# SSM inputs brought into step order: one wide copy and transfers through DRAM in place of sixteen small copies a chunk

## The chip, the cores and the metric

The kernel runs on one core of one Trainium2 chip. The metric is the device time of one execution in microseconds. The core's engines run side by side, each through its own queue of instructions in order: TensorE (PE in the profile, PEld for its weight loads), VectorE (DVE), ScalarE (ACT), GpSimd (POOL) and SyncE (SP), which here only issues transfers (DMA). An engine waits at an instruction until what it needs is there, and everything behind it on that queue waits too.

## What is computed

One decoder block over 512 tokens of width 1024: a conditioned norm, one combined input projection, differential attention beside a diagonal state space model (SSM), gates, an output projection, and a mixture of 32 experts. The change lies in the SSM branch; cut to it, the reference is:

```python
h = modulate(rms_norm(x, norm1_g), shift1, scale1)
q, k, v, u, gates = split(h @ w_in)            # u: (512 tokens, 512 channels)
ug = u.reshape(1, 512, 32, 16)                 # 32 groups of 16 channels
bu = einsum('bsgh,gph->bsgp', ug, bb)          # complex, 64 states a group
x_t = a * x_(t-1) + bu_t                       # scan over the 512 tokens, per state
y = Re(einsum('bsgp,ghp->bsgh', x, c)) + d_skip * ug
y = gelu(y); gl = y @ w_glu
y_ssm = gl[:, :512] * sigmoid(gl[:, 512:])
merged = g_attn * (y_attn @ w_proj_attn) + g_ssm * (y_ssm @ w_proj_ssm)
```

## The kernel before

The 512 SSM channels are worked on in four chunks `c` of 128. The SSM goes four tokens at a time: token 4b + q is step q of block b, with 128 blocks. For that the input of a chunk has to lie in "step order": the tile `us` (`U[c]`, 128 x 4 x 128) has in partition 32q + h channel h of a quarter of the chunk at step q, and in its free part the quarter j and the block b. The input projection leaves u differently: channel on the partition, tokens in order along the free part, in the PSUM tiles `acc` 0 to 3. `ssm_u(c)` (line 415) does the rearrangement with 16 copies of 32 x 128 on ScalarE (line 420), each reading every fourth token. Chunk 0 is read straight from PSUM; chunks 1 to 3 are first copied into SBUF tiles `u1` to `u3` (line 574).

`ssm_steps` (line 704) then takes each chunk through these steps: `ssm_rotate` (matmuls `bu` of `us` with `W`, line 652, then the products `m` and sums `z` on VectorE with tables `cos` and `sin`), `ssm_in` for the next chunk (its `ssm_u`, then transposes `bt` on TensorE, line 428, and copies `W` on ScalarE, line 429), `ssm_scan`, `ssm_back` (`xri`) and, one chunk later, `ssm_y` (matmuls `yp`, lines 692 and 694, the latter reading `us` again; then a table load and 16 GELU instructions `yf`, line 698). `us` has two buffers, so chunk c + 2 can be filled only when `yp` of chunk c has been computed. `table` builds `cos` and `sin` for the next chunk on VectorE and ScalarE.

Beside this TensorE works through the rest of the input projection: `acc` (line 180; q, k) and value matmuls `vps` (line 185), whose weights arrive as `ws` (line 145, 512 KB each), are cast by ScalarE to `wh` (line 153), and the remainder `wl` is formed by VectorE (a line 90). Every few matmuls a "tick" runs one SSM step or one unit of the second conditioning product (`ada_unit`): a 512 KB transfer `adaw` (line 747) and 8 matmuls `mvb` (line 749). Units 0 to 15 use two buffers of `adaw`, later ones four; every eighth unit ends with a VectorE step `mr` and a small transfer `mrd`. `tv` (line 768), `tvd` and `bsd` (lines 770 and 772) build the table of attention biases through DRAM; `bsd` is 1 MB from DRAM to DRAM, and `B` (line 777) reads it.

From line 566 on a scheduler decides the order of the instructions on each engine, up to the attention stage, where TensorE's order is written out by hand. Its order is fixed when the program is built; the transfers of SP are one queue in that order too.

```python
uT = [acc[0]]
for c in range(1, 4):
    uT.append(t1(f"u{c}", [128, T]))
    S.copy(uT[c], acc[c])
    if c == 1:
        ssm_u(0)
```

Of the kernel before, what the change touches and what calls it, by code (L numbers as in the profile page):

```python
# [9 lines left out]
F32 = mybir.dt.float32  # L10
# [9 lines left out]
T, D = 512, 1024  # L20
# [37 lines left out]
def hybrid_block(ctx: ExitStack, tc: tile.TileContext, x, cols, cst, ada_a, ada_b, b_rows, bc_rows, lamv, relb,  # L58
                 onehot, units, rw, rb, bpad, cpad, w_ein, w_eout, out):
    nc = tc.nc  # L60
    V, S, G, TE = nc.vector, nc.scalar, nc.gpsimd, nc.tensor
# [3 lines left out]
    dram = ctx.enter_context(tc.tile_pool(name="dram", bufs=1, space=DRAM))  # L65

    def bank(i, shape=(128, 512), name=None):
        return psum.tile(list(shape), F32, tag=f"b{i}", name=name or f"bank{i}")
# [8 lines left out]
    def t1(tag, shape, dt=F32, name=None):  # L77
        pool = late if tag[:-1] == "tmp" else mid if tag[:-1] in ("BT", "CT", "sgA", "xs") else early
        return pool.tile(list(shape), dt, tag=tag, name=name or tag)
# [116 lines left out]
    def two(i, name):  # L196
        if i == 0:
            return [bank(0, name=name), bank(1, name=name)]
        t = pair(name=name)
        return [t[:, 0], t[:, 1]]  # L200
# [114 lines left out]
    v, y, t = (st4[:, j] for j in range(3))  # L315
# [97 lines left out]
    U, W = {}, {}  # L413

    def ssm_u(c):

        U[c] = t1(f"v{c % 2}", [128, 4, 128], name="us")
        for j in range(4):
            for q in range(4):
                S.copy(U[c][32 * q:32 * q + 32, j], uT[c][32 * j:32 * j + 32, q::4])  # L420

    def ssm_w(c, ps):

# [95 lines left out]
    with tc.manual_schedule(engines={mybir.EngineType.PE, mybir.EngineType.DVE, mybir.EngineType.Activation}):  # L519
# [4 lines left out]
        acc = two(0, "acc0") + two(1, "acc2") + [bank(m, name=f"acc{m}") for m in (4, 5)]  # L524
# [11 lines left out]
        for k in range(KC):  # L536
            first, second = unit_parts(UNITS[k]) if k in UNITS else (lambda: None, ) * 2
            for n in range(3 * 6):

                m, w = (n // 2, n % 2) if n < 12 else (n - 12, 2)  # L540
                b = 6 * k + m
# [26 lines left out]
    for _ in setup:  # L568
        pass

    uT = [acc[0]]
    for c in range(1, 4):
        uT.append(t1(f"u{c}", [128, T]))
        S.copy(uT[c], acc[c])
        if c == 1:
            ssm_u(0)
    qT, kT, vt = [None] * 4, [None] * 4, [None] * 4

# [61 lines left out]
    def ssm_in(c):  # L640
        if c:
            ssm_u(c)
            ps = pair((128, 2, 4, 128), "bt")
            ssm_w(c, [ps[:, ri] for ri in range(2)])
# [325 lines left out]
    for i in range(4):  # L970
        m2s = []
        for m in (2 * i, 2 * i + 1):
# [6 lines left out]
            b = t1(f"u{2 + m % 2}", [128, T], name="mb")  # L979
# [5 lines left out]
        for j in range(2):  # L985
            cs = slice(256 * i + 128 * j, 256 * i + 128 * j + 128)
            v = m2s[j].rearrange("p (i t) -> p i t", t=128)
# [826 lines left out]
```

## Time and profile before

| | |
|---|---|
| median of 3 runs | 939.51 us (938.96 to 942.91) |
| the profiled execution | 938.94 us, its span 937.1 us |
| TensorE busy | 893.2 us (95% of the span), 4967 matmuls |
| VectorE busy | 502.0 us (54%) |
| ScalarE busy | 300.3 us (32%), 616 instructions |
| GpSimd busy | 2.2 us |
| moved by DMA | 268.70 MB, mean 287 GB/s |
| 61.5 to 200 us | the SSM beside q, k, v and the conditioning |
| 200 to 323 us | attention with gates between |
| 450 to 921 us | experts |

Busy shares are means over stages of very different kinds: in the experts' stage TensorE is busy 468.0 of 471 us. What counts for a change in one stage is which waits end last there. Matmuls are pipelined, so the busy time of TensorE contains no small gaps; a wait that shows is a real one. The granted clock of TensorE is given as a share of 2.4 GHz.

### The profile page before, as it was taken

Reading aid. Unit: us, or ns where it says so; the run is one execution under the profiler, and the core shown is the slowest. Engines: PE = TensorE matmul, PEld = TensorE weight load, DVE = VectorE, ACT = ScalarE, POOL = GpSimd, SP = SyncE. Lnnn points to the kernel's source line nnn. Section 1 sums busy time; section 2 is a strip of 40 time slices with the busy share of each in tenths; the row PEclk is TensorE's granted clock in tenths of the full one; section 3 lists DMA queues with packets and bytes.
Section 4 is the critical chain, followed back from the end, with each engine's and each line's share of the span. In section 5 each row is a group of like instructions: output and inputs, shape, how many; then the busy total and the mean of one; then the engine's idle time right before and its main releaser. Section 6 shows DMA issues by size and latency. Waiting matters only on the chain.

```text
span 937.1 us, 12889 instructions
## 1 busy us (share of the span) xinstructions
PE 893.2 (95%) x4967; PEld 554.4 (59%) x4967; DVE 502.0 (54%) x1256; ACT 300.3 (32%) x616; POOL 2.2 (0%) x8
## 2 busy tenths in 40 slices
PE   8997997889999999999999999999999999999994
PEld 4775765567778788778455543555435554355343
DVE  7896685656765557469524432544225442244336
ACT  4565568895644433243201000010000100001014
POOL 0000000000000000000000000000000000000000
PEclk9998999999999999999999999999999999999998
DMA  9925765612222623691899999999999999999952
GB/s 362 376 82 175 253 219 194 218 55 86 68 68 69 220 94 126 262 376 40 343 379 417 420 420 420 420 420 420 420 420 420 420 420 419 420 420 420 419 174 93
DMA packets 77590, 268.70 MB, mean 287 GB/s; under 512 B 5535, under 2 KB 11567, under 8 KB 77524
## 3 DMA queue, kind: packets, MB, share of 16 engines
q1 hardware_dynamic: 77524, 267.82, 72.9%
q8 instruction: 41, 0.67, 0.3%
q14 instruction: 25, 0.20, 0.1%
HBM read 265.68 MB, written 3.17 MB: 287 GB/s over the span
## 4 chain that ended last, share of the span: by engine, by line
PE 83%; ACT 6%; DVE 6%; DMA 3%; issue 1%; SPq 0%; DVEq 0%; ACTq 0%
PE hid L1412 23%; PE yb L1419 11%; PE acc L180 11%; PE cb L1397 7%; PE xg L1155 6%; PE pAS L180 5%; PE po L185 4%; PE acc L543 4%; DMA adaw<-ada_b 3%; ACT us L420 3%; PE plg L180 2%; ACT yf L698 2%; PE pv L864 1%; PE lp L1088 1%; PE mv L474 1%
## 5 line engine op out<-in xcount | busy, mean ns | idle before, releaser
L1412 PE MATMUL hid<-w,xT 128*64 128x512 f32 x1024 | 222.9, 592 | 0.0
L1412 PEld LDWEIGHTS hid<-w,xT 128*64 128x64 f32 x1024 | 73.3, 137 | 145.3 <-issue 136.5
L1419 PE MATMUL yb<-w,sa 128*64 128x512 f32 x480 | 106.3, 595 | 0.0
L90 DVE TENSOR_TENSOR sa<-sa,hid 128x512 f32<-128x512 f32 (+1 forms) x17 | 11.1, 656 | 166.3 <-PE hid L1412 153.9
L90 DVE TENSOR_TENSOR wl<-ws,wh 128x1024 fp32r<-128x1024 f32 x52 | 63.5, 1223 | 56.1 <-ACT wh L153 45.4
L90 DVE TENSOR_TENSOR x<-x,cb 128x512 f32<-128x512 f32 (+1 forms) x132 | 79.9, 664 | 2.0 <-PE cb L1397 2.0
L153 ACT ACTIVATE wh<-ws 128x1024 fp32r<-128x1024 f32 x51 | 53.7, 1057 | 80.0 <-PE acc L180 24.5
L180 PE MATMUL acc<-hh,wh 128*128 128x512 f32 x176 | 74.1, 421 | 4.4 <-ACT wh L153 4.4
L1390 ACT CAST yh<-yf 128x512 fp32r<-128x512 f32 x29 | 17.9, 619 | 172.0 <-DVE yf L96 141.7
L1419 PEld LDWEIGHTS yb<-w,sa 128*64 128x64 f32 x480 | 33.2, 137 | 65.0 <-issue 64.4
L180 PE MATMUL acc<-hl,wh 128*128 128x512 f32 x176 | 70.9, 403 | 0.0
L180 PE MATMUL acc<-hh,wl 128*128 128x512 f32 x176 | 70.6, 402 | 0.0
L1377 ACT ACTIVATE sa<-hid 128x512 f32<-128x512 f32 x15 | 9.0, 597 | 177.0 <-PE hid L1412 177.0
L96 DVE SCALAR_TENSOR_TENSOR yf<-yb,ws,gate 128x512 f32<-128x512 f32 x29 | 21.8, 751 | 80.8 <-PE yb L1419 80.3
L1155 PE MATMUL xg<-P,mh 128*128 128x256 f32 x224 | 54.7, 284 | 0.0
L1155 PE MATMUL xg<-P,ml 128*128 128x256 f32 x224 | 53.5, 280 | 0.0
L1397 PE MATMUL cb<-yh,PT 128*128 128x512 f32 x116 | 48.2, 416 | 0.4 <-ACT yh L1390 0.3
L1397 PE MATMUL cb<-yl,PT 128*128 128x512 f32 x116 | 45.9, 396 | 2.1 <-DVE yl L90 2.0
L1155 PEld LDWEIGHTS xg<-P,ml 128*128 128x128 f32 x224 | 42.2, 189 | 0.5
L1155 PEld LDWEIGHTS xg<-P,mh 128*128 128x128 f32 x224 | 42.1, 188 | 0.5
L180 PEld LDWEIGHTS acc<-hh,wh 128*128 128x128 f32 x176 | 33.7, 191 | 14.1 <-ACT wh L153 4.6
L180 PEld LDWEIGHTS acc<-hh,wl 128*128 128x128 f32 x176 | 33.5, 190 | 9.4 <-issue 1.6
(316 smaller groups left out, 1441.3 us busy)
## 6 DMA issues: line engine op xcount, KB each, us to landing
w<-w_ein SPq DMA_DIRECT2D x128, 1024.0 KB, 13.3
w<-w_eout SPq DMA_DIRECT2D x63, 1024.0 KB, 17.5
ws<-units SPq DMA_DIRECT2D x52, 512.0 KB, 3.6
adaw<-ada_b SPq DMA_DIRECT2D x32, 512.0 KB, 4.5
ada<-ada_a SPq DMA_DIRECT2D x8, 512.0 KB, 8.2
ada<-ada_a SPq DMA_DIRECT2D x16, 256.0 KB, 7.1
X<-x SPq DMA_DIRECT2D x4, 512.0 KB, 6.4
x<-x SPq DMA_DIRECT2D x4, 512.0 KB, 5.5
```

The source lines that it names most:

```text
L90: return emit(o, lambda: (eng or V).tensor_tensor(o, a, b, op=op))
L96: return emit(o, lambda: V.scalar_tensor_tensor(o, a, s, b, op0=op0, op1=op1, **k))
L153: return (lambda: S.activation(hi, st, AF.Copy) if u else V.tensor_copy(hi, st)), lambda: tt(lo, st, f32(hi), OP.subtract)
L180: TE.matmul(o, a, b, start=start and i == 0, stop=stop and i == 2)
L185: TE.matmul(o, a, b, start=start and i == 0, stop=stop and i == 2)
L420: S.copy(U[c][32 * q:32 * q + 32, j], uT[c][32 * j:32 * j + 32, q::4])
L543: TE.matmul(acc[m], (hi, lo, hi)[w], hT(k)[w // 2], start=k == 0 and n < 12 and w == 0, stop=k == KC - 1 and w == 2)
L698: S.activation(f[32 * j:32 * j + 32, p::4], yp[32 * p:32 * p + 32, j], AF.Gelu_apprx_tanh)
L1155: TE.matmul(o, (h2h, h2l)[w][i][:, 128 * k:128 * k + 128], P[:, i].rearrange("p a b -> p (a b)"), start=start, stop=i == NT - 1 and w == 1 ...
L1397: TE.matmul(ps, PT if len(y) == 2 else f32(PT), a, start=w == 0, stop=w == len(y) - 1)
L1412: m = TE.matmul(hid[q][64 * e:64 * e + 64], xT[p, k // 4][:, k % 4, 64 * e:64 * e + 64], ring[p][k][:, e, 512 * q:512 * q + 512], start=k ...
L1419: TE.matmul(yb[q][64 * e:64 * e + 64], hT_[:, f, 64 * e:64 * e + 64], ring[p][8 + f][:, e, 512 * q:512 * q + 512], start=f == 0, stop=f == ...
```

## The change

`ssm_u` no longer copies. After the projection each chunk, chunk 0 now too, is copied once from PSUM to an SBUF tile `u` with the tokens regrouped by step (128 x 512, read with a step of four). ScalarE issues a 256 KB transfer of it into a DRAM tile `ud`. `ssm_u(c)` is four 64 KB transfers on SP's queue, one for each step q, which read the 32 channels of all four quarters from DRAM in runs of 128 elements into the 32 partitions of `us` that belong to q.

```diff
     def ssm_u(c):
 
         U[c] = t1(f"v{c % 2}", [128, 4, 128], name="us")
-        for j in range(4):
-            for q in range(4):
-                S.copy(U[c][32 * q:32 * q + 32, j], uT[c][32 * j:32 * j + 32, q::4])
+        v = ud[c].rearrange("(j h) (q b) -> q h j b", h=32, b=128)
+        for q in range(4):
+            nc.sync.dma_start(U[c][32 * q:32 * q + 32], v[q])
...
-    uT = [acc[0]]
-    for c in range(1, 4):
-        uT.append(t1(f"u{c}", [128, T]))
-        S.copy(uT[c], acc[c])
-        if c == 1:
+    ud = []
+    for c in range(4):
+        u_ = t1(f"u{c}", [128, T], name="u")
+        S.copy(u_.rearrange("p (q b) -> p q b", q=4), acc[c].rearrange("p (b q) -> p q b", q=4))
+        ud.append(dram.tile([128, T], F32, name=f"ud{c}"))
+        nc.scalar.dma_start(ud[c], u_)
+        if c == 0:
             ssm_u(0)
```

The scheduler puts this together anew. ScalarE's queue right after the input projection stands before the change as (`us` from `acc_281` is chunk 0, from `u_866` chunk 1; `wh_919` and `wh_1029` are the first two weight tiles of the next projections):

```order
L420 COPY us<-acc_281 32x128 x4
L574 COPY u_866<-acc_282 128x512
L420 COPY us<-acc_281 32x128 x12
...
L420 COPY us<-u_866 32x128 x6
L768 COPY tv<-tvp 4x320
L420 COPY us<-u_866 32x128 x10
L919 ACT_TABLE_LOAD
L919 ACTIVATE lmt<-lmt 128x2
L581 ACTIVATE q_1024<-acc 128x512
L768 COPY tv<-tvp 4x320
L153 ACTIVATE wh_919<-ws_917 128x1024
L153 ACTIVATE wh_1029<-ws_1027 128x1024
```

After the change the same place reads as follows (`ud_868` to `ud_885` are the stores of chunks 0 to 3):

```order
L574 COPY u<-acc_281 128x512
L574 COPY u<-acc_282 128x512
L576 DMA ud_868<-u 128x512
L576 DMA ud_877<-u 128x512
L574 COPY u<-acc_283 128x512 x2
...
L576 DMA ud_881<-u 128x512
L576 DMA ud_885<-u 128x512
L770 COPY tv<-tvp 4x320
L921 ACT_TABLE_LOAD
L921 ACTIVATE lmt<-lmt 128x2
L583 ACTIVATE q_1010<-acc 128x512
L770 COPY tv<-tvp 4x320
L153 ACTIVATE wh_917<-ws_915 128x1024
```

The 32 small copies are gone from in front of the second `tv` and of `wh`, and two pairs of transfer issues stand there.

SP's queue at the same time, before the change, from the transfers of conditioning units 2 and 3 on:

```order
L747 DMA adaw<-ada_b 128x1024 x2
L145 DMA ws_917<-units 128x1024
L145 DMA ws_1027<-units 128x1024
L770 DMA tvd<-tv 4x640
L747 DMA adaw<-ada_b 128x1024 x2
L145 DMA ws_1110<-units 128x1024
L772 DMA bsd<-tvd 512x1x512
```

And after it:

```order
L749 DMA adaw<-ada_b 128x1024 x2
L420 DMA us<-ud_868 32x4x128 x4
L420 DMA us<-ud_877 32x4x128 x4
L145 DMA ws_915<-units 128x1024
L145 DMA ws_1013<-units 128x1024
L772 DMA tvd<-tv 4x640
L749 DMA adaw<-ada_b 128x1024 x2
L145 DMA ws_1096<-units 128x1024
L774 DMA bsd<-tvd 512x1x512
```

Eight loads of `us` now stand between the two `adaw` and the weight tiles.

TensorE's queue at `yp` of chunk 1, in the second stage, before (the `mvb` x4 and x12 are conditioning units 16 and 17 to 19):

```order
L692 MATMUL yp<-xri,CA 128x128 x2
L749 MATMUL mvb<-adaw,c_94 32x256 x4
L694 MATMUL yp<-us,G 128x128
L749 MATMUL mvb<-adaw,c_94 32x256 x12
L428 MATMUL bt<-colt,BE 128x128 x4
L692 MATMUL yp<-xri,CA 128x128 x2
L694 MATMUL yp<-us,G 128x128
L692 MATMUL yp<-xri,CA 128x128 x2
L694 MATMUL yp<-us,G 128x128
```

And after (the last `mvb` x4 here is unit 20):

```order
L751 MATMUL mvb<-adaw,c_94 32x256 x12
L428 MATMUL bt<-colt,BE 128x128 x4
L696 MATMUL yp<-us,G 128x128
L694 MATMUL yp<-xri,CA 128x128 x2
L696 MATMUL yp<-us,G 128x128
L694 MATMUL yp<-xri,CA 128x128 x2
L751 MATMUL mvb<-adaw,c_94 32x256 x4
L696 MATMUL yp<-us,G 128x128
```

A block of `mvb` has moved to just ahead of the last matmul of `yp`. Elsewhere in this part the order of ScalarE and VectorE is nearly what it was.

## Rows read from the trace of the kernel before

**Rows 1.** Windows by stage: length, then busy time (instructions) of each engine, clock, DMA.
```profile
61.50:105.90 44.40, 37.80 (x227) 26.28 (x226) 31.00 (x67) 25.27 (x55) 0.00 (x0) 0.92 0.58 208
...
132.90:157.00 24.10, 17.44 (x134) 12.29 (x133) 12.14 (x19) 20.50 (x41) 0.00 (x0) 1.00 0.44 148
157.00:178.00 21.00, 16.89 (x97) 12.11 (x95) 13.98 (x24) 20.34 (x42) 0.00 (x0) 0.92 0.64 227
178.00:200.00 22.00, 18.71 (x144) 12.86 (x144) 18.21 (x28) 19.19 (x39) 0.00 (x0) 0.97 0.42 157
200.00:323.00 123.00, 122.75 (x597) 97.65 (x595) 72.19 (x241) 67.01 (x152) 0.00 (x0) 0.99 0.28 94
```

**Rows 2.** TensorE's waits from 61.5 to 200 us: total us, times, longest.
```profile
PE acc L180 <- ACT wh L153: 4.4, 1, 4.4
PE bu L652 <- ACT W L429: 4.1, 1, 4.1
PE bt L428 <- DVE m L90: 3.6, 2, 2.3
PE sc L837 <- DVE qs L90: 3.2, 2, 2.8
PE mvb L749 <- DMA adaw<-ada_b: 2.9, 3, 1.5
PE yp L692 <- ACT yf L698: 1.6, 1, 1.6
PE mvb L749 <- DVE mr L90: 1.3, 1, 1.3
```

**Rows 3.** Line 420: count, ns minimum/median/maximum, first and last start.
```profile
L420 ACT COPY us<-u x48: 408/418/447, 69.3 to 163.6; 32x128 f32<-32x128 f32 x48
L420 ACT COPY us<-acc x16: 252/256/260, 62.5 to 67.1; 32x128 f32<-32x128 f32 x16
```

**Rows 4.** Timeline of the first stage: start us, length us, what, idle before.
```profile
63.53 0.59 ACT L574 COPY u<-acc 128x512 f32<-128x512 f32 x1
...
71.84 0.70 PE L767 MATMUL tvp<-oht,rbt 33*4 33x320 f32 x2
...
78.50 0.40 ACT L768 COPY tv<-tvp 4x320 f32<-4x320 f32 x1
...
78.81 2.00 ACT L153 ACTIVATE wh<-ws 128x1024 fp32r<-128x1024 f32 x2
...
80.63 0.67 SPq L772 DMA_DIRECT2D bsd<-tvd  x1
...
98.07 0.33 SPq L777 DMA_DIRECT2D B<-bsd  x1
```

**Rows 5.** Waits of SP's queue from 60 to 205 us.
```profile
SPq L770 <- ACT tv L768: 12.9, 1, 12.9
```

**Rows 6.** Timeline of ScalarE in the second and third stage.
```profile
132.94 6.93 ACT L420 COPY us<-u 32x128 f32<-32x128 f32 x16 [0.53 <-PE yp L694]
...
157.08 6.92 ACT L420 COPY us<-u 32x128 f32<-32x128 f32 x16 [0.76 <-PE yp L694]
...
170.53 0.59 ACT L429 COPY W<-bt 128x512 f32<-128x512 f32 x1
171.14 1.20 ACT L698 ACTIVATE yf<-yp 32x128 f32<-32x128 f32 x3
```

**Rows 7.** Transfer issues: count, KB each, median us from issue to landing.
```profile
ws<-units SPq DMA_DIRECT2D x52, 512.0 KB, 3.6
adaw<-ada_b SPq DMA_DIRECT2D x32, 512.0 KB, 4.5
...
colt<-cols SPq DMA_DIRECT2D x1, 107.5 KB, 2.0
```

**Rows 8.** Windows of 3 us, columns as in rows 1.
```profile
81.00:84.00 3.00, 1.69 (x7) 1.25 (x6) 3.00 (x6) 0.43 (x1) 0.00 (x0) 0.50 0.96 367
```

**Rows 9.** The chain that ended last, in order of time: start us, length us.
```profile
108.59 6.30 PE acc L180 x27
```

## The prediction

> **What bounds the kernel now.** I first read the windows by stage, for where TensorE is not kept busy [rows 1]. From 200 us on it is (122.75 of 123.00 us in the attention stage). Between 61.5 and 200 us it idles 6.6 us before 105.9, 6.7 us from 132.9 to 157, 4.1 us to 178 and 3.3 us to 200, and its granted clock falls to 0.92 in two of these stretches. So only this front part can give time, and what it gives passes on, since all that follows is released by work that moves with it.
>
> TensorE's waits there have seven entries [rows 2]. Five lead to ScalarE or to something queued behind it: acc on wh (4.4 us), bu on W (4.1), yp on yf (1.6), mvb on mr (1.3; on VectorE mr stands behind wl, which waits for wh), bt on m (3.6 in two waits, 1.3 and 2.3; m stands behind the cosine table and, the first time, behind lmt, both ScalarE results). The other two are sc on qs (3.2) and mvb on adaw transfers (2.9 in three waits, the longest 1.5).
>
> The copies of line 420 are 16 x 0.256 us and 48 x 0.418 us, 24.2 us of ScalarE [rows 3]. In the first stage 32 of them lie between the end of the input projection and the second copy of tv, at 78.50 us, and wh follows at 78.81 [rows 4]. SP, which issues its transfers in order, waited 12.9 us for that tv [rows 5]: nothing was loaded meanwhile. In the second and third stage 16 copies each, 6.93 and 6.92 us, stand directly ahead of the table load and yf [rows 6].
>
> **The change, part by part.** It removes 24.2 us from ScalarE. It adds one 128x512 copy (u of chunk 0; the three others were there, 0.59 us each [rows 4]) and four transfer issues on ScalarE's queue. No strided 512-element copy out of PSUM is in the trace: between 0.59 us (contiguous) and four times 0.256 (four strided quarters, 1.02) I take 0.6, since the quarters each hold an instruction's fixed part. No transfer is issued by ScalarE either; zero and 1.3 us (four times SP's) bound one issue, SP's 0.33 us [rows 4] is taken. That is 0.6 + 1.3 = 1.9 us: net 22 us of ScalarE freed.
>
> It also adds sixteen loads of 64 KB to SP's queue. The first eight stand, by the order, ahead of ws_915, ws_1013 and tvd; the first of them waits until chunk 0's store has landed. A landing takes 2.0 us at the shortest and 4.5 us for an adaw [rows 7]. The copy of chunk 1 ends at 64.1 us now, behind four small copies [rows 4]; with one wide copy in their place the first store goes out at about 64 and lands at 66 to 68.5. Eight issues of 0.33 us, and waits for the stores of chunks 2 and 3 (issued at about 67, behind two copies and two q), let ws go out at 70.5 to 73. With 3.6 us to land [rows 7] and 1.0 us to cast [rows 4], wh is ready at 75 to 77.5 instead of 79.8.
>
> *Stage one, 61.5 to 105.9 us.* tv's second copy loses 32 copies (10.8 us) from in front of it, but its matmuls run until 72.5 [rows 4], so it moves only from 78.50 to about 72.2, 6.3 us. The burst of transfers behind it (adaw, ws, bsd) moves with it, less the ws pair that now goes out just ahead: 1 MB at the burst's 367 GB/s [rows 8] is 2.9 us, of which I count 1.2, since until tv is there SP waits in any case. That is 5.1 us. From TensorE's side the stage gives 4.4 + 1.3 us of waits and up to 3.6 us for the clock (0.08 of 44.4 us [rows 1]; 0.50, the 1.2 GHz level, is granted from 81 to 84 us, right after the long wait [rows 8]): 5.7 to 9.3. TensorE cannot run ahead of adaw, so the smaller side decides: **5.5 us** taken, 2.7 (slow landings) to 7.7 the bounds.
>
> *Stage two, 132.9 to 157 us.* The copies leave; yf starts after yp and its table load, 6.9 us earlier, and with it wh, wl, mr, the cosine table and m. TensorE's waits on yf, mr and the second on m go: 1.6 + 1.3 + 2.3 = 5.2 us. Late next is adaw: by the order a block of mvb now stands ahead of the last matmul of yp, its transfer queued behind ws and mr. Nothing shows this wait; it lies between zero and 4.5 us (a whole landing), and I take 1.5, the longest wait on adaw that there is. Chunk 2's own input is covered: SP issues its loads when yp of chunk 0 ends, and 27 value matmuls (6.3 us, as 27 acc of the same shape take [rows 9]) and two blocks of mvb come ahead of bu. Without that cover bu would wait 2.0 to 4.5 us and four issues. **3.7 us**, 0 to 5.2.
>
> *Stage three, 157 to 178 us.* 6.92 us leave ahead of yf. W, which ran at 170.53 ahead of the last three yf (1.20 us [rows 6]), now runs behind all 16, still 5.7 us earlier. bu's wait of 4.1 us goes, and of the clock (0.08 of 21 us, 1.7) I count 1.4. **5.5 us**, 2 to 5.8. Behind SP's wait for yp stand B and the next adaw, whose buffers come free later than yp ends: nothing lost.
>
> *178 to 200 us.* The way from yf of chunk 2 over the kd casts to sc is ScalarE work that the change leaves alone: **0**, from -1 to +2.8 (if adaw comes early, sc's wait shrinks).
>
> Sum: 5.5 + 3.7 + 5.5 = 14.7 us. The profiled run took 938.94 us (span 937.1 and 1.8 around it), 0.6 below the median of 939.51 and as fast as the fastest run. 938.94 - 14.7 = 924.2; on the median 924.8. I say **924.5 us**.
>
> The copies that read SBUF with a step of four elements took 0.418 us, those that read PSUM 0.256 [rows 3]. The Trainium skill (ScalarE: Activation LUTs, What ACT_TABLE_LOAD costs) gives an instruction with immediate operands as 186 ns plus 0.833 ns an element, an estimate of 0.293 us for either; the trace does not agree. By it 16 copies would be 4.7 us instead of 6.9, stages two and three would each give up to 2.2 us less, and the time would be about 929; the measured rows decide.
>
> **Rivals.** *The transfers of adaw become the bound.* For: TensorE already waits for them three times [rows 2], and each of the first 16 units has one of two buffers, so a unit cannot be asked for before the one two ahead has been used. Against: the stretch moves 148 to 227 GB/s, the burst 367 [rows 1, 8], and the change adds 2 MB. Price: stage two's 3.7 and 4.2 of stage one's 5.5 are lost, 938.9 - 6.8 = **932 us**.
>
> *The relay is late.* If each of the four loads of a chunk pays its landing by itself, one after the other, 4 x 2.0 = 8 us and more pass from the free buffer to bu, longer than the 6.9 us of copies. Then stage one gives nothing and the two others lose about 2 us each: 938.9 - (3.7 + 5.5 - 4) = **934 us**, 936 with slower landings. Against it: an issue of SP is over after 0.33 to 0.67 us [rows 4], long before the landing, so the four overlap. Of the Trainium skill, the rule in DMA: Bandwidth & Descriptors (Rules for kernel authors) that many small transfers should be merged, as under 64 KB one pays mostly overhead, speaks for this rival; no run here shows such a load yet.
>
> *Slower: SP's queue is held.* tvd, ws and adaw stand behind eight loads that wait for a store. bsd, a transfer with DRAM at both ends, was issued at 80.63, and B, which reads it, went out only at 98.07 [rows 4]: 17.4 us. If the store and the load each took that, wh would come near 104 us, 24 us later than now, and with 9.2 us gained in stages two and three the run would take about **953 us**. It decides against the change from a round trip of some 16 us on; 4 to 9 us is what two landings say.
>
> *No difference.* ScalarE's time was only cover, and VectorE or adaw would have held TensorE at the same places: **938 us**. Against it: yp waits on yf and bu on W, both ScalarE's own [rows 2].
>
> **How the numbers follow.** The forecast (up to 930 us) gets 0.67, adaw as the bound 0.18, the late relay 0.07, no difference 0.03, the held queue 0.05. A measurement of this kernel can tell 0.5% (4.7 us) from no change, so faster means below 934.8. The late relay lies at that edge and counts as no change: faster 0.85, same 0.10, slower 0.05. The upper bounds of all terms (7.7 + 5.2 + 5.8 + 2.8 = 21.5) give 917.4; the range goes from 918 to 933 and takes in the adaw case.
>
> **What would show it.** Right: tv's second copy near 72 us; wh at 75 to 77.5; the granted clock at 1.0 from 75 to 90 us; yf right behind yp, and bu no longer waiting for W; attention scores some 15 us earlier, and the stages after them as long as before. Wrong: a ScalarE issue well over 0.33 us, the first us landing after 73, TensorE waiting over 3 us in sum for us or adaw. A gain in stages two and three without one in stage one would mean that SP is held; a front that is shorter and an end that is not would refute that the rest moves with it.

## The result

The change is faster by about 1%: 929.64 us (median of 4 runs, 927.95 to 930.01) against 940.28 of the kernel before (4 runs), a ratio of 0.988 with a 95% interval of 0.9854 to 0.9906. In a second group of runs it took 930.22 against 938.88, ratio 0.9904 (0.9891 to 0.9916). The gain is some 10.6 us of the 14.7 that were forecast: the time lies in the range, 5.1 us above the forecast and 2.4 us below the rival in which the transfers of adaw become the bound (932). The likeliest outcome had been given as "up to 930 us"; the two medians stand on either side of that edge.

The windows by stage of the changed kernel (length, then busy time and instructions of PE, PEld, DVE, ACT, POOL, then clock, DMA share, GB/s) answer [rows 1]:

```profile
61.50:105.90 44.40, 41.28 (x242) 28.34 (x241) 36.51 (x75) 16.89 (x26) 0.00 (x0) 0.92 0.83 280
...
132.90:157.00 24.10, 21.36 (x159) 15.02 (x157) 16.62 (x26) 17.89 (x37) 0.00 (x0) 1.00 0.71 233
...
200.00:323.00 123.00, 122.45 (x597) 97.57 (x598) 76.70 (x249) 62.24 (x139) 0.00 (x0) 1.00 0.32 107
```

TensorE still idles 3.1 us in the first window and 2.7 in the second, and the clock of the first is 0.92, as it was. The waits of TensorE from 61.5 to 200 us (total, times, longest) answer [rows 2]:

```profile
PE mvb L751 <- DMA adaw<-ada_b: 5.6, 4, 1.7
PE sc L839 <- DVE qs L90: 2.4, 2, 1.2
PE acc L180 <- ACT wh L153: 1.5, 2, 1.0
PE wtp L856 <- DVE pp L96: 0.7, 1, 0.7
```

W, yf, m and mr are gone from the list; wh is down from 4.4 to 1.5 us. In their place adaw has risen from 2.9 to 5.6. Of ScalarE's timeline in the first stage, two rows that answer [rows 4], then of SP's, and one of TensorE's:

```profile
71.75 0.41 ACT L770 COPY tv<-tvp 4x320 f32<-4x320 f32 x1
75.92 1.06 ACT L153 ACTIVATE wh<-ws 128x1024 fp32r<-128x1024 f32 x1 [3.75 <-DMA ws<-units]
```

```profile
65.25 6.73 SPq L420 DMA_DIRECT2D us<-ud  x8
72.08 0.86 SPq L145 DMA_DIRECT2D ws<-units  x2
73.07 0.28 SPq L772 DMA_DIRECT2D tvd<-tv  x1
73.45 1.20 SPq L749 DMA_DIRECT2D adaw<-ada_b  x2
```

```profile
80.67 1.08 PE L751 MATMUL mvb<-adaw,c 128*32 128x256 f32 x8 [1.57 <-DMA adaw<-ada_b]
```

These are the times that the prediction named: tv's second copy near 72, ws out between 70.5 and 73, wh between 75 and 77.5. Two of its other signs came out against it. TensorE was not to wait over 3 us in sum for us or adaw; it waits 5.6 us for adaw, and in the first stage adaw, asked for at 73.45, was used only at 80.67, after a wait of 1.57 us. And the granted clock was to be 1.0 from 75 to 90 us; it fell all the same, as the windows from 79.5 us show (0.50 is the 1.2 GHz level; TensorE had stood idle for 1.02, 0.53 and 1.57 us since 76.0):

```profile
79.50:81.00 1.50, 0.33 (x4) 0.20 (x8) 1.50 (x3) 0.00 (x0) 0.00 (x0) 0.50 0.83 339
...
84.00:85.50 1.50, 1.50 (x5) 1.21 (x4) 1.32 (x2) 0.15 (x1) 0.00 (x0) 0.50 0.77 152
```

**A ruler for the stages.** On every engine the instructions of the first 60 us are the same in all kernels here (but for the first load of mr, where the mr loads go out from GpSimd's queue), yet they do not take the same time in every execution: the first bt begins at 60.3 to 64.2 us in the fourteen profiles. Most of this goes with the granted clock: in the six profiles with bt at 60.3 to 60.6 us it is 1.00 throughout, in the six at 61.6 to 62.3 it is 0.91 over the first 20 us, and in the one at 64.2 it is 0.87 and 0.96 over the first and second 20 us; only mr_load_on_pool (62.8, clock 1.00) falls out. So the stages are compared by the time from that bt to marks on TensorE: the last pair of yp<-us of each chunk, and the first sc. Rows of TensorE's timeline, before:

```profile
60.45 1.04 PE L428 MATMUL bt<-colt,BE 128*128 128x128 f32 x8
...
132.51 0.39 PE L694 MATMUL yp<-us,G 128*128 128x128 f32 x2
...
156.65 0.39 PE L694 MATMUL yp<-us,G 128*128 128x128 f32 x2
...
182.52 0.39 PE L694 MATMUL yp<-us,G 128*128 128x128 f32 x2
```

The same of the changed kernel:

```profile
60.52 1.04 PE L428 MATMUL bt<-colt,BE 128*128 128x128 f32 x8
...
129.86 0.49 PE L696 MATMUL yp<-us,G 128*128 128x128 f32 x2
...
150.71 0.49 PE L696 MATMUL yp<-us,G 128*128 128x128 f32 x2
...
171.97 0.39 PE L696 MATMUL yp<-us,G 128*128 128x128 f32 x2
```

From bt to the mark of chunk 0 it was 72.06 us and is 69.34: 2.7 gained. To chunk 1, 96.20 and 90.19: 6.0. To chunk 2, 122.07 and 111.45: 10.6. To the end of the span (937.1 and 926.2) 11.1. The table has the gains of all kernels by this ruler, each worked out from such rows of its own trace, which is one execution; the medians are of all runs:

| gain in us at | yp 0 | yp 1 | yp 2 | sc | end of span | median us |
|---|---|---|---|---|---|---|
| change | 2.7 | 6.0 | 10.6 | 12.9 | 11.1 | 929.64 |
| change_again | 2.2 | 4.4 | 9.0 | 11.3 | 9.8 | 930.22 |
| relay_in_old_order | 3.7 | 10.6 | 15.4 | 15.4 | 14.1 | 924.89 |
| tensor_old_order | 3.0 | 4.5 | 10.4 | 10.4 | 10.1 | 928.41 |
| copies_in_new_order | -1.0 | -4.4 | -7.6 | -5.3 | -7.0 | 946.86 |
| relay_chunks_0_1 | 4.8 | 1.9 | -3.1 | -2.7 | -2.9 | 946.21 |
| relay_0_1_in_old_order | 5.6 | 5.5 | 5.6 | 5.6 | 4.8 | 937.03 |
| relay_chunks_2_3 | 1.6 | 3.0 | 6.2 | 4.6 | 4.6 | 935.41 |
| us_loads_on_pool | 6.6 | 11.4 | 14.4 | 8.8 | 8.7 | 930.89 |
| us_on_pool_held | 6.3 | 9.3 | 14.3 | 16.6 | 13.2 | 926.39 |
| half_adaw_held | 8.3 | 13.1 | 18.3 | 20.6 | 18.2 | 921.56 |
| mr_load_on_pool | 3.1 | 6.9 | 12.9 | 15.2 | 13.8 | 927.27 |
| old_order_pool_queue | -2.8 | 4.3 | 8.7 | 8.7 | 7.0 | 929.92 |

The kernel before had medians of 940.49, 940.20 and 938.88 in the three groups of runs below.

### The profile page after: what moved, and what is told of

The parts are those of the page before. It is cut to its first block, busy times and chain, and to the rows that moved or that the text cites. A ratio compares the mean times of both kernels' runs of the same rounds, so it can differ in the third digit from the quotient of the medians.

```text
span 926.2 us, 12858 instructions
## 1 busy us (share of the span) xinstructions
PE 891.8 (96%) x4967; PEld 552.1 (60%) x4967; DVE 502.1 (54%) x1256; ACT 277.0 (30%) x553; POOL 2.2 (0%) x8
## 4 chain that ended last, share of the span: by engine, by line
PE 85%; DVE 7%; ACT 4%; DMA 3%; issue 1%; SPq 0%; DVEq 0%; ACTq 0%
PE hid L1414 24%; PE acc L180 11%; PE yb L1421 11%; PE cb L1399 7%; PE xg L1157 6%; PE pAS L180 5%; PE po L185 4%; PE acc L543 3%; DMA adaw<-ada_b 2%; PE plg L180 2%; ACT yf L700 2%; PE vps L185 1%; PE mvb L751 1%; PE pv L866 1%; PE lp L1090 1%
## 5 line engine op out<-in xcount | busy, mean ns | idle before, releaser
L90 DVE TENSOR_TENSOR sa<-sa,hid 128x512 f32<-128x512 f32 (+1 forms) x17 | 11.1, 656 | 166.3 <-PE hid L1414 153.9
```

Of the source, the lines that this page charges most:

```text
L90: return emit(o, lambda: (eng or V).tensor_tensor(o, a, b, op=op))
```

## Experiments

### The relay, or the order that the planner makes of it

A planner sets the order of all instructions, and any edit makes it set them anew. To part the two, an experiment adds edges of issue order (no waits) between neighbours on an engine, so that what both kernels have stands in a given order. ORDER lists the instructions of four engines by number, each as its distance from the one before it:

```diff
+ORDER = (
+    "245 1 1 1 1 1 1 1 1 1 ...",
...
+def hold(nc, tc, edge):
+    here = {i.name: i for i in nc.cur_bb.bb.instructions}
+    for row in ORDER:
+        n, last = 0, None
+        for step in row.split():
+            n += int(step)
+            i = here.get(f"I-{n}")
+            if i is None:
+                continue
+            if last is not None:
+                tc.add_manual_dep(i, last, edge, reason="order")
+            last = i.name
...
-    xs = [per.tile([128, D], F32, name=f"x1_{i}", tag=f"X{i}") for i in range(NT)]
+    hold(nc, tc, mybir.DependencyInfo(mybir.DependencyClass.NoSync, mybir.DependencyReason.DATA)); xs = [...]
```

**relay_in_old_order** is this with ORDER from the kernel before, in the changed kernel.

> The change, but TensorE, VectorE, ScalarE and SP are held to the order of the kernel before (the small copies taken out, the relay's transfers put in where the planner finds room). The prediction was worked out on the old order and gave 924.5. Theory A (the planner's new order is part of the gain, since it puts bu of the last chunk and the casts earlier): this kernel keeps less than the change, 932 to 936. Theory B (the new order costs what is missing): it comes out at 924 to 927, below the change's 929.6.

Measured: 924.89 us (5 runs), ratio 0.9842 (0.9818 to 0.9866): theory B. In the old order the relay is worth 15.3 us, and the planner's new order gives back about 5 (929.64 and 930.22; the interval of the latter, 0.9891 to 0.9916, lies apart). Its marks on TensorE, and its waits from 61.5 to 200 us:

```profile
61.60 1.04 PE L428 MATMUL bt<-colt,BE 128*128 128x128 f32 x8
...
130.01 0.39 PE L696 MATMUL yp<-us,G 128*128 128x128 f32 x2
...
147.25 0.39 PE L696 MATMUL yp<-us,G 128*128 128x128 f32 x2
...
168.33 0.39 PE L696 MATMUL yp<-us,G 128*128 128x128 f32 x2
```

```profile
...
PE mvb L751 <- DMA adaw<-ada_b: 2.7, 2, 1.8
PE bu L654 <- DMA us<-ud: 1.6, 1, 1.6
PE bt L428 <- DVE m L90: 0.9, 1, 0.9
```

The mark of chunk 1 stands 85.65 us after bt, that of the change 90.19: the second stage is where the new order costs. The window of that stage, here and (above) in the change:

```profile
132.90:157.00 24.10, 23.90 (x174) 16.63 (x172) 19.37 (x31) 20.77 (x40) 0.00 (x0) 1.00 0.74 230
```

0.2 us idle against 2.7. (In change_again the granted clock of this window is 0.93, not 1.00, which goes with its still smaller gain there.) In the change, mvb waits twice there for adaw, in front of the last pairs of yp of chunk 1:

```profile
145.03 1.50 PE L751 MATMUL mvb<-adaw,c 128*32 128x256 f32 x24 [1.06 <-DMA adaw<-ada_b]
...
150.15 0.64 PE L751 MATMUL mvb<-adaw,c 128*32 128x256 f32 x8 [1.68 <-DMA adaw<-ada_b]
```

**copies_in_new_order** is the reverse: the kernel before, ORDER from the changed one.

> The kernel before, with its small copies, but TensorE, VectorE, ScalarE and SP held to the order of the changed kernel (the copies go where the planner finds room). Theory A (part of the gain is order alone): below 940, at 935 to 938. Theory B (the gain is ScalarE's time; the new order needs it): 940 or slower, up to 946, since the new order was made for a ScalarE without the copies.

Measured: 946.86 us, ratio 1.0073 (1.0059 to 1.0087): theory B again, just beyond its far end (946). The order is no gain in itself; it needs a ScalarE without the copies. With them TensorE waits for what now stands behind them:

```profile
PE mvb L749 <- DVE mr L90: 7.1, 1, 7.1
PE bu L652 <- ACT W L429: 6.0, 1, 6.0
PE acc L180 <- ACT wh L153: 4.0, 1, 4.0
```

**change_again** is the changed kernel, unedited.

> The changed kernel once more, beside the three others: 929.6 as before, 928 to 931. It tells how much of the 4.7 us between it and relay_in_old_order (924.9, of another group of runs) is noise.

Measured: 930.22 us (929.05 to 931.14). The difference to relay_in_old_order is not noise.

**tensor_old_order** holds TensorE's row of ORDER alone.

> The change with TensorE alone held to the old order; the planner places the rest. Theory (the 4.7 us lie in TensorE's order, where blocks of mvb stand ahead of their transfers): 925, as relay_in_old_order. Rival (they lie in the order of VectorE and ScalarE): 928 to 930.

Measured: 928.41 us, ratio 0.9882 (0.9868 to 0.9897): the time of the rival, though its cause was not tried by itself. With TensorE in the old order and the rest planned anew, its waits for adaw are longer than in the change (5.6 us) and in relay_in_old_order (2.7):

```profile
PE mvb L751 <- DMA adaw<-ada_b: 7.3, 4, 3.3
```

So at most some 2 of the 5 us lie in TensorE's order by itself. The rest must lie in the orders on SP, VectorE and ScalarE, or in how TensorE's fits them; the waits point to the order in which SP asks for adaw, but which of the three carries it was not tried.

### Stage by stage

**relay_chunks_0_1** and **relay_chunks_2_3** relay two chunks each; the planner sets the order.

```diff
     def ssm_u(c):
...
+        if c not in (0, 1):
+            for j in range(4):
+                for q in range(4):
+                    S.copy(U[c][32 * q:32 * q + 32, j], uT[c][32 * j:32 * j + 32, q::4])
+            return
...
+        if c in (0, 1):
+            u_ = t1(f"u{c}", [128, T], name="u")
...
+        elif c:
+            uT[c] = t1(f"u{c}", [128, T])
+            S.copy(uT[c], acc[c])
```

The other has (2, 3) in both places.

> Chunks 0 and 1 go through DRAM as in the change, chunks 2 and 3 by the 16 small ScalarE copies of before. In the trace of the changed kernel TensorE's first yp stands 3.3 us earlier than before, and 10.9 us of the whole are gained. If the stages add up (theory: each stage's gain is its own), this kernel keeps about 3 us of the gain: 940.3 - 3 = 937. If instead the earlier start of the first stage is what later stages gain from (rival), it keeps most of it: 931 to 933.

> Chunks 2 and 3 go through DRAM, chunks 0 and 1 by small copies. Theory (the stages' gains add up): 7 to 8 us stay, 932.5. Rival (all hangs on the first stage): 937 or more. The first stage is to show again the wait of SP for tv of some 13 us and TensorE's wait for wh of over 4 us.

Measured: 946.21 us (941.32 to 948.09; the profiled execution took 941.99), ratio 1.0049 (1.0032 to 1.0067), slower than before; and 935.41, ratio 0.9944 (0.9923 to 0.9965), between theory and rival. Neither theory nor rival of the first has a relay of two chunks that costs time, and the two do not add up to the change. The ruler shows that the first gains 4.8 us in its stage and loses 8 by chunk 2. TensorE's waits for adaw and yf are longer than in the kernel before (2.9 and 1.6 us), though chunks 2 and 3 are copied here as they were there:

```profile
PE mvb L762 <- DMA adaw<-ada_b: 8.3, 3, 5.1
PE yp L705 <- ACT yf L711: 5.0, 2, 3.1
```

The second still has SP's wait for tv, 12.1 us, as expected, but not the wait for wh: TensorE waits 2.2 us there, for a copy of u.

**relay_0_1_in_old_order** repeats the first with the order of the kernel before.

> Chunks 0 and 1 by the relay, 2 and 3 by small copies, as relay_chunks_0_1 (945), but TensorE, VectorE, ScalarE and SP held to the order of the kernel before. Theory (the planner's order is what made that kernel slow): the first stage's term of the prediction alone, 940.3 - 5.5 = 935, 933 to 937. Rival (relayed early chunks do harm in the later stages whatever the order): 943 or more.

Measured: 937.03 us (12 runs, 934.58 to 939.23), ratio 0.9979 (0.9965 to 0.9992). It is no longer slow, so the loss was the planner's order. On the ruler its gain is 5.5 to 5.6 us at every mark from chunk 0 to sc: the prediction's first term, and nothing after it. By the medians it is about 2 us, less than in its profile (935.68 us in all, 3.3 below the profile of before); the rest lies in the time before bt, 61.80 us against 60.45, and after sc.

### What holds the first stage

**us_loads_on_pool** moves the loads of us from SP's queue to GpSimd's.

```diff
-            nc.sync.dma_start(U[c][32 * q:32 * q + 32], v[q])
+            nc.gpsimd.dma_start(U[c][32 * q:32 * q + 32], v[q])
```

> The changed kernel, with the 16 loads of us issued by GpSimd's queue, not SP's. In the changed kernel ws of the second projection was issued at 72.08 us, behind the eighth load of us. Theory (the us loads hold SP, so ws, tvd and adaw are late): ws goes out near 65 us, TensorE's 1.5 us for wh and most of its 1.6 us for adaw at 80 go, 929.6 - 3 = 926.6; if the 6.8 us at half clock from 78.8 us go with the waits, another 3.4 us, 923. Rival (VectorE or the landing of us bounds the first stage): 929.6 or, with slower loads from this queue, above it.

Measured: 930.89 us, ratio 0.9893 (0.9871 to 0.9915), no better than the change: the rival's time, but not the rival's reason. On the ruler it is far better up to chunk 2 (14.4 us against 10.6) and gives the lead back at chunk 3: the planner had put that chunk's yp ahead of its input.

```profile
PE yp L694 <- DVE xri L90: 7.1, 2, 6.2
```

**us_on_pool_held** has the same edit with ORDER from the changed kernel on all four engines.

> As us_loads_on_pool, but with TensorE, VectorE, ScalarE and SP held to the changed kernel's order. The planner had put yp of the last chunk ahead of its input there, and TensorE waited 6.2 us at 184. Theory (the us loads hold SP and make the first stage late): without that give-back 929.6 - 3 to 6 = 924 to 927, with the first stage at full clock. Rival (the first stage's gain does not reach the end because adaw and VectorE set the pace of the later stages): 929 to 930.

Measured: 926.39 us, ratio 0.9859 (0.9844 to 0.9874): 3.2 us below the change, as the theory's first figure. Waits of TensorE from 61.5 to 200 us, the window of the first stage, and SP's issue of the first two ws:

```profile
PE mvb L751 <- DMA adaw<-ada_b: 4.8, 4, 1.5
PE sc L839 <- DVE qs L90: 2.4, 2, 1.2
PE bu L654 <- DMA us<-ud: 0.7, 1, 0.7
```

```profile
61.50:105.90 44.40, 42.73 (x259) 29.97 (x258) 38.02 (x79) 19.92 (x38) 4.46 (x8) 1.00 0.85 299
```

```profile
64.97 1.56 SPq L145 DMA_DIRECT2D ws<-units  x2
```

ws goes out at 64.97 us and not at 72.08, wh no longer appears, the clock stays at 1.00, and the first stage gains 6.3 us, not 2.7. So in the change the us loads do hold SP. How, the program tells: the transfers that SP and ScalarE issue share eight completion semaphores in turn, so that each waits until the eighth before it has landed. SP's instructions at this place, numbered, with the semaphores that each waits for (DMAHW0 to DMAHW7 are the eight, PE and DVE an engine's own):

```
48 L749 DMA adaw<-ada_b 128x1024 [waits DMAHW7_49,DMAHW1_49,PE_49]
49 L749 DMA adaw<-ada_b 128x1024 [waits DMAHW2_49,DMAHW0_49,PE_49]
...
54 L420 DMA us<-ud_877 32x4x128 [waits DMAHW1_49]
55 L420 DMA us<-ud_877 32x4x128 [waits DMAHW2_49]
56 L420 DMA us<-ud_877 32x4x128 [waits DMAHW3_49]
57 L420 DMA us<-ud_877 32x4x128 [waits DMAHW4_49]
58 L145 DMA ws_915<-units 128x1024 [waits DMAHW5_49,DVE_49]
```

The fifth and sixth load of us wait for the two adaw issued just ahead of them, 1 MB that has nothing to do with them. In the waits of SP's queue from 62 to 84 us of the change:

```profile
SPq L420 <- DMA adaw<-ada_b: 2.5, 2, 1.7
```

In relay_0_1_in_old_order, where the stores of chunks 2 and 3 do not take two of the eight, the same loads go out in 5.03 us, not 6.78 as in relay_in_old_order, and the first stage gains 5.6 us, not 3.7 (one execution each). The Trainium skill (DMA: Bandwidth & Descriptors, Rules for kernel authors) says that spreading transfers over several issuing engines brings no bandwidth and saves only issue time. No run here measures bandwidth by itself, but the loads were no faster: they took longer to land from GpSimd's queue (median 6.1 us, 5.0 from SP's). On the second the runs show more than the issue time: what was gained is the queue behind the loads, which had stood 2.5 us for adaw.

**half_adaw_held** halves the conditioning loads, with ORDER from the changed kernel; half of the conditioning rows are left out, and TensorE's work is the same.

```diff
-        nc.sync.dma_start(st, ada_b[i])
+        nc.sync.dma_start(st[:, :512], ada_b[i][:, :512])
...
-            TE.matmul(mvb[r][32 * j:32 * j + 32], c32[:, k], st[:, 256 * j:256 * j + 256], start=k == 0, stop=k == KC - 1,
+            TE.matmul(mvb[r][32 * j:32 * j + 32], c32[:, k], st[:, 256 * (j % 2):256 * (j % 2) + 256], start=k == 0, stop=k == KC - 1,
```

> The changed kernel in its own order, with each conditioning load halved to 128x512, and the same half used twice by the matmuls: half of the conditioning rows are left out, TensorE's work is unchanged. Theory (the adaw transfers bound what is left): TensorE's 5.6 us of waits for adaw go, 929.6 - 4 to 5 = 925; with the clock that falls after the wait at 80 us, another 3.4 us. Rival (they are late by SP's queue, not by their size): the waits go by a third or so, 928.

Measured: 921.56 us, ratio 0.9805 (0.9791 to 0.9818): 8.1 us below the change, the theory with its clock. TensorE's waits from 61.5 to 200 us:

```profile
...
PE mvb L751 <- DMA adaw<-ada_b: 1.9, 3, 0.8
```

In this order the bytes of adaw are worth 8 us of the whole: the rival "adaw becomes the bound" had come true in part. Not all of it is TensorE's own wait: by the ruler 5.6 us of it come in the first stage, where the eight us loads, which wait for two adaw, now go out in 5.08 us and not 6.73. The two effects are not parted here.

**mr_load_on_pool** moves only the four loads of mr to GpSimd's queue.

```diff
-            nc.sync.dma_start(mr, _ap(b_rows, r * D, [[256, 4], [0, 32], [1, 256]]))
+            nc.gpsimd.dma_start(mr, _ap(b_rows, r * D, [[256, 4], [0, 32], [1, 256]]))
```

> The changed kernel, with the four loads of mr (L755) issued by GpSimd's queue, not SP's. In the changed kernel SP stood 2.8 and 1.9 us between the store mrd and the load of the next mr, with adaw behind it, and TensorE then waited 1.7 and 1.3 us for these adaw. Theory (adaw is late because SP is held by mr): both waits go, 929.6 - 2.5 to 3 = 927. Rival (adaw is late because its buffers come free late or because a transfer takes 4.4 us anyhow): the waits stay, 929.6 within 0.5.

Measured: 927.27 us (924.93 to 932.10), ratio 0.9866 (0.9837 to 0.9896). The median fits the theory, but the interval reaches over the change's ratio of 0.988, so the runs alone do not settle it. The traces do for the waits: in the change SP stands from 142.23 to 145.02 for the store of mrd, with adaw behind it,

```profile
141.70 0.53 SPq L757 DMA_DIRECT2D mrd<-mr  x1
145.02 0.56 SPq L755 DMA_DIRECT2D mr<-b_rows  x1
145.68 0.42 SPq L749 DMA_DIRECT2D adaw<-ada_b  x1
```

and TensorE's waits for adaw fall from four (5.6 us) to two. The two that the theory named (1.7 and 1.3 us) are gone; the one ahead of them in the second stage has grown from 1.06 to 2.31 us, so that stage gains little by it:

```profile
PE mvb L751 <- DMA adaw<-ada_b: 3.2, 2, 2.3
```

```profile
148.14 1.50 PE L751 MATMUL mvb<-adaw,c 128*32 128x256 f32 x24 [2.31 <-DMA adaw<-ada_b]
```

### All together

**old_order_pool_queue**: both GpSimd edits in the old order.

> The change in the old order, with the loads of us and of mr issued by GpSimd's queue. If the three effects add up (order 4.7, mr 2.4, us on GpSimd 3.2 as in us_on_pool_held): 940.3 - 10.6 - 10.3 = 919.4. If they are the same waits counted twice: 924 to 925.

Measured: 929.92 us (927.01 to 935.70), ratio 0.9894 (0.9879 to 0.9909): neither; 5 us worse than the old order alone. The profiled execution took 935.70, the longest of the five, and its first bt began 3.7 us later than that of the kernel before, so what it shows is an indication only. In the old order the second half of tvp stands behind bu of chunk 0, and bu now waits longer for us (3.2 us, 1.6 in relay_in_old_order); so tv, for which SP holds tvd and adaw, comes late. tvd goes out 16.0 us after bt (14.4 in relay_in_old_order), and TensorE's longest wait for adaw is 4.7 us (1.8). Waits of TensorE, and SP's row:

```profile
PE mvb L751 <- DMA adaw<-ada_b: 5.6, 2, 4.7
PE bu L654 <- DMA us<-ud: 3.8, 2, 3.2
```

```profile
80.14 0.27 SPq L772 DMA_DIRECT2D tvd<-tv  x1
```

What helps the new order, where tvp stands ahead of bu, harms the old one; which of the two edits does so was not tried. The lowest median of a kernel that computes the whole reference remains that of relay_in_old_order.

## Why the prediction was partly right

**What bounds the kernel.** Right: the front gives time, and ScalarE's copies were what held it. "No difference" (938) is refuted. That the front's gain passes on to the end is right too: the span after 200 us is as full as before. The relay in the old order takes 924.89 us, and 924.5 was forecast, but that is in part luck: by stages it gave 3.7, 6.9 and 4.8 us, not 5.5, 3.7 and 5.5.

**Prices of the new instructions.** Right. The wide strided copy takes 0.59 us (0.6 taken), a transfer issue of ScalarE 0.34 to 0.37 (0.33), the first stage's SP times fit to within a microsecond.

```profile
L574 ACT COPY u<-acc x4: 587/590/593, 62.5 to 64.5; 128x512 f32<-128x512 f32 x4
L576 ACTq DMA_DIRECT2D ud<-u x4: 335/348/367, 63.2 to 65.1; - x4
```

**Stage one, 5.5 us; measured 2.7 and 2.2.** The first step that failed. SP's side moved as worked out: tvd from 78.92 to 73.07 us, 5.9 (6.3 taken). But of the burst "I count 1.2", and it cost more: adaw, asked for at 73.45, was used at 80.67, 7.2 us later, not the 4.5 of [rows 7], as two ws went out just ahead of it and us loads were still landing. In us_on_pool_held, where these ws had gone out at 64.97, adaw was asked for at 72.53 and used at 77.86, without a wait. TensorE's side came out short too. 5.7 us of waits and up to 3.6 us of the clock had been counted; its idle time in the window fell by 3.5, from 6.6 to 3.1 us, since wh still cost it 1.5 us and adaw 1.6 (0.9 before), and of the clock nothing came back (0.92 in both). With the us loads on GpSimd's queue, in the same order, the stage gave 6.3; with two chunks relayed, in the old order, 5.6. So the size was right for a relay that does not hold SP. The hold of some 6.7 us was in the sum, and ws went out when it was said to; that two of the loads wait for adaw, and that ws and adaw then land together, was not.

**Stage two, 3.7 us; measured 3.3 and 2.2.** Near in sum, by two errors. In the old order the stage gives 6.9 us (10.6 - 3.7): more than the upper bound of 5.2, since with the copies gone no wait at all was left there, the one on adaw included. In the planner's order mvb waits 1.06 and 1.68 us, 2.7 where 1.5 was taken. The step that failed is the comparison of the orders: "nearly what it was" was said of ScalarE and VectorE, one block of mvb was priced, and the rest was costed as if it stood as before. By the whole times it costs about 5 us between two kernels with the same work, more than the 4.1 by which the gain fell short: stage two in the old order gave more than was forecast.

**Stage three, 5.5 us; measured 4.6 and 4.7.** Right in mechanism: bu no longer waits for W. 4.8 in the old order.

**178 to 200 us, 0; sc came 2.3 us more early.** It was of no use. The first softmax's exp stands behind the last chunk's sixteen yf on ScalarE, and yf followed yp, not sc; VectorE waited for it:

```profile
DVE sm L848 <- ACT pp L847: 6.2, 1, 6.2
```

**Rivals.** The adaw case (0.18, 932) is the one that the result lies next to, though not by its cause alone: with the bytes halved the time falls 8.1 us, with the old order and all bytes it falls about 5. The held queue (953) was right as a mechanism and far off in price, some 3 us and not 24. The late relay did not happen as written (the loads overlap), though bu of chunk 0 begins at 73.37 us; it was 70.85 before.

**What stays open:** why stage two of the old order is free of waits for adaw and that of tensor_old_order is not; which engine's order carries the 5 us; and, since each kernel has one profile, how much of the small differences between stages is the execution and not the kernel.

## What to carry to other kernels

Where a planner sets the order, hold the old order with edges of issue order and measure an edit twice, in the old and in the planner's: here the edit was worth 15.3 us and the new order gave back 5. Many small transfers cost places in flight on the queue (here eight, shared with ScalarE's); count what stands behind them, and whose landing they wait for. A wait that is gone shows the next one: price that one from a burst as it will be, not from a median landing.

## Not expected of the hardware

A ScalarE copy of 128x512 from PSUM, read with a step of four elements, takes 0.59 us, as long as a contiguous one, while a 32x128 copy with the same step, a quarter of its elements a partition, had cost 0.256 [rows 3]. The sixteen loads of 64 KB took 5.0 us to land in the median (2.0 to 6.4), the first eight of them with two loads of 512 KB just ahead; the four stores of 256 KB, issued from ScalarE just before, from 63.15 us on, took 2.4. With adaw halved the loads took 3.8.
